# Second layer's first 512 MLP features by seven half-size products, with the first two products of three groups in the seam

## The chip, the cores and the metric

One core of one Trainium2 chip runs the whole program. The metric is the device time of one execution in microseconds (us). Differences of under 0.2% (1.6 us here) are not told from no change.

## The reference, cut to what matters

Two decoder layers work on 512 tokens of width 1024 in float32. Each has a mixer, a norm with a modulation that is computed from `c`, and an MLP of 4096 features. The second layer's mixer is a gated unit (called SGU below) that ends with the product by `sgu_w_out`. The change concerns the way from there into the second layer's MLP:

```python
def sq_relu_mlp(h, w1, w2):
    return jnp.square(jax.nn.relu(h @ w1)) @ w2
...
        x = x + g1[:, None, :] * y                                # y = gated @ w_out in layer 2
        h = modulate(rmsnorm(x, norm_mlp_g[i]), sh2, sc2)
        x = x + g2[:, None, :] * sq_relu_mlp(h, mlp_w1[i], mlp_w2[i])
```

## The kernel before

**Three products for one.** TensorE (PE) multiplies in a reduced float32 format. Each operand is split into a high part and a remainder (`wh`/`wl` for weights, two `hb` or `as` halves for activations), and a product is the sum of three matmuls (`mm3`, L558): `wl` by high, `wh` by remainder, `wh` by high, in this order for each slice of 128 inputs. So the second matmul of a product already needs the remainder of the activations. A weight split (`split`) is one ACT copy (`wh`) and one DVE subtraction (`wl`). `split_d` makes `wl` by two ACT copies and an accumulating DMA from POOL's queue in place of the subtraction; the list `LO` names the weights that are done so.

**The MLP's first matrix** is computed in eight groups of 512 features, called (c, j). A group is done either plainly (eight input slices, 512 tokens, 128 features at a time), or by seven half-size products (`s_prep`, `s_run`), the Winograd form of Strassen's scheme: inputs, features and tokens are halved, and each product m = 1 to 7 takes 512 inputs, 256 features and 256 tokens, that is 24 matmuls of 128x256. Products 1, 2 and 4 use plain quarters of the activations. Products 5, 6, 3 and 7 use sums of quarters (`a_parts`) that take both token halves. DVE builds them from `h32`, which holds the normed activations with features on partitions; then each is split into two halves (`as` or `hb`, function `parts`: an ACT copy and a DVE subtraction). The weights of 5 and 6 are running sums in `tr` (DVE adds the block `rg` or `yr`). The accumulators are evicted to `g` by ACT (`g<-po`) or DVE (`g<-g,po`), then squared by ACT.

**The seam.** The last product of the mixer (`sgu_w_out`) is done for the token tiles 0, 1, 2 and then 3. After tile 2, `normed(0, 1, 1)` turns the first two token tiles: 16 transposes into four `px` banks, DVE and ACT scale them into `h32` (`h<-px`, one half of each bank each), then `parts` makes `hb`. After tile 3 the same follows for the second token half, `normed(1, 1, 1)`, as soon as its sums of squares are there: DVE adds into `x`, ACT squares, DVE adds up (`sums`), POOL takes the power (`rr`), DVE and ACT scale rows (`xs`). Meanwhile PE needs work on the first token half alone. In the kernel before this is `first1` (L1818): the second layer's first group is done plainly, in halves of 256 tokens, four times 24 matmuls on the first half, with the second `normed` within them, then four times 24 on the second half. The other seven groups follow by seven products each (`FROM[1] = 1`), the first of them in `ORDER1`.

**What sets the order.** PE's order is the program's. All other engines' orders are made by a planner (`Plan.run`) which replays the recorded operations with its own costs and writes each engine's queue; so an edit of one stage can reorder DVE, ACT, POOL and SP from where it is first felt. Every recorded operation therefore has one line in the profile, L128. An engine works its queue strictly in that order.

**Buffers that matter:** `gq`, eight tiles of 8 KB for `g`, gates and modulation columns (`ada`); `w4`, three raw weight tiles; five pairs `wh`/`wl`; PSUM with four banks in pool `ps` (`px`, most `po`) and four in `xz`.

Of the kernel before, what the change touches and what calls it, by code (L numbers as in the profile page):

```python
# [14 lines left out]
P = 128  # L15
# [407 lines left out]
@with_exitstack  # L423
def decoder_kernel(ctx: ExitStack, tc: tile.TileContext, xtok, vecs, fgrow, ada0, ada1, pool_w, w1s, w1, w1f, w1b, w2, w_v, w_u, w_o, wsT, ws, bs, out):
    nc = tc.nc
# [106 lines left out]

    LO = "o0 o1 u5 u7 v41".split()

# [520 lines left out]

    ORDER1 = (1, 2, 5, 6, 3, 7, 4)

# [11 lines left out]

    FROM = (3, 1)  # L1070

    def mlp(i, first, extra, last, ending):
# [3 lines left out]
        if True:  # L1076
            g, y_ = {}, []
            early = [gq.tile([P, 2, D], F32, name="rg", tag="g")] if FROM[i] < 3 - i else []

# [26 lines left out]
            def f_prep(u):  # L1106
                c, f = u
                return split(raw4(w1[8 * c + f] if i == 0 else w1f[8 * c + f]))

# [11 lines left out]

            sums_a = {}

            x32 = h32[0] if i else xf

            def a_parts(step):


                def a(r, j):
                    return x32[:, 4 * j : 4 * j + 4, 256 * r : 256 * r + 256]  # L1130

                def operand(pool, tag):
                    o = pool.tile([P, 2, 4, 256], F32R, name="as", tag=tag)
                    return o[:, 0], o[:, 1]

                if step == 0:
                    first, half = slice(0, 256), slice(256, 512)
                    sums_a.update({1: H(slice(0, 4), first), 2: H(slice(4, 8), first), 4: H(slice(4, 8), half)})
# [18 lines left out]
            def blk(c, j, r, n):  # L1157
                if (c, j, r, n) not in blks:
                    q = quad_at(c, j) - quad_at(*first_quad)
                    if (r, n) == (1, 0):  # L1160
                        o = w4.tile([P, D], F32, name="raw", tag="w4")
                    elif (r, n) == (0, 0):
                        o = (chained or chained.append(hx.tile([P, 2, D], F32, name="tr", tag="t0")) or chained)[0][:, q % 2]
                    elif q == 0 and early:
                        o = early[0][:, r]
                    else:
                        o = (pieces or pieces.append(ytile("yr")) or pieces)[0][:, 2 * (q % 2) + r]
# [7 lines left out]
            def s_prep(u):  # L1175
# [22 lines left out]
                more = {1: [(c, j, 0, 1), (c, j, 1, 1)], 5: [(*nxt, 0, 0)], 6: [(c, j, 1, 0)], 3: [(*nxt, 0, 1)], 7: [(*nxt, 1, 1)]}.get(m, [])  # L1198
                for at in more:
# [6 lines left out]
            def s_run(u, w):  # L1206
# [5 lines left out]
                if start:  # L1212
                    banks[:] = [bank("po")]
                po = banks[0].rearrange("p (a t) -> p a t", a=2)
                wv = w[0].rearrange("p (k c) -> p k c", k=4), w[1].rearrange("p (k c) -> p k c", k=4)
                for f in range(2):
                    for k in range(4):
                        mm3(po[:, f], cut(wv, ALL, k, slice(P * f, P * f + P)), apart(cut(sums_a[m], ALL, k)), start and f + k == 0, stop and f + k == 4, skip_group_check=True)

# [157 lines left out]

            done = first(put)
            units = [("f", divmod(f, 8)) for f in range(done, 4 * FROM[i])]
            at = []  # L1380
            for q in range(FROM[i], 8):
                units += [("s", (*divmod(q, 2), m)) for m in (ORDER1 if q == FROM[i] < 3 - i else ORDER)]
                at.append(len(units) - 1)
# [76 lines left out]
    def normed(hf, i, n, xs=None, ks=range(0, KD, 2)):  # L1460
# [3 lines left out]
        for k in ks:  # L1464
# [5 lines left out]
            for q in range(2):  # L1470
# [346 lines left out]

    def first1(put):  # L1818
        n = 4
        wf = [split(raw4(w1f[f]), 1 if f else 4) for f in range(n)]  # L1820
        wf = [(h.rearrange("p (k c) -> p k c", k=KD), l.rearrange("p (k c) -> p k c", k=KD)) for h, l in wf]
        pos = [bank("po", xz) for _ in range(n)]
        for hf in range(2):
            c = slice(256 * hf, 256 * hf + 256)
            for f in range(n):
                if hf == 0 and f < 2:
                    mm3_late(pos[f][:, c], [cut(wf[f], ALL, k) for k in range(KD)], [apart(H(k, c)) for k in range(KD)])
                    continue
                for k in range(KD):
                    mm3(pos[f][:, c], cut(wf[f], ALL, k), apart(H(k, c)), k == 0, k == KD - 1)  # L1830
                    if (hf, f, k) == (0, n - 2, LATE):
                        normed(1, 1, 1)
                        spill(1)
        for f in range(n):
            put(f, pos[f].rearrange("p (r c) -> p r c", r=2))
        return n

    fgb = []
# [28 lines left out]

    ex = [x for q in range(8) for x in modulation_late(48 + q, 6 + 4 * q, late_gb if q == 0 else get_gb)]
    ex += [(49, lambda: spread_cols(mods[1][:, c_g(1, 0) : c_g(1, 0) + KD], "gain1"))]
    mlp(1, first1, ex, last1, lambda: None)  # L1870
    plan.run(LEAD)

# [12 lines left out]
def _lay_out(inp):  # L1885
# [35 lines left out]
    d["w1"] = fmajor(w1[0][:, : 3 * S], P)  # L1921
    d["w1f"] = fmajor(w1[1][:, : 1 * S], P)

    w1b = np.concatenate([w1[0][:, 3 * S :], w1[1][:, 1 * S :]], axis=1)
    d["w1b"] = w1b.reshape(2, 4, P, 12, 2, 256).transpose(3, 0, 4, 2, 1, 5).reshape(12, 2, 2, P, D)

# [27 lines left out]
```

## Time and profile before

| | |
|---|---|
| time, median of 3 runs | 800.47 us (799.83 to 800.86) |
| the profiled execution | 800.96 us |
| its span in the trace | 799.3 us |
| granted TensorE clock, mean | 0.994 |
| DVE busy | 690.7 us, 86% of the span |
| ACT busy | 531.7 us, 67% |
| seam: last matmul by `sgu_w_out` starts | 491.61 us |
| seam: second `normed`, 16 transposes start | 499.53 us |
| seam: first product with a sum of quarters (5) starts | 520.37 us |

The profile lists for each instruction its start, its length and, in brackets, how long its engine idled before it and what ended that. Successive instructions of one engine overlap a little, so the pitch from start to start counts as what one costs its engine. Matmuls of 128x256 read 0.27 us each but follow each other every 0.11 us.

### The profile page before, as it was taken

How to read it: one execution, taken by the hardware profiler on the slowest of the kernel's cores; microseconds unless marked ns; L12 is line 12 of the kernel's file. 1: busy time of each engine (PE TensorE's matmuls, PEld its weight loads, DVE VectorE, ACT ScalarE, POOL GpSimd, SP SyncE). 2: the span in 40 equal slices, each digit the busy share in tenths (PEclk: the TensorE clock that was granted, in tenths of full speed). 3: DMA queues.
4: the chain of work that ended last, by engine and by line, in shares of the span. 5: the costliest groups of instructions: out<-in, count | busy, mean ns of one | idle time of the engine just before them, and what ended most of it. 6: DMA issues, size and time to landing. Idle time of an engine off the chain costs nothing.

```text
span 799.3 us, 12696 instructions
## 1 busy us (share of the span) xinstructions
PE 781.3 (98%) x4893; PEld 708.4 (89%) x4893; DVE 690.7 (86%) x898; ACT 531.7 (67%) x768; POOL 106.3 (13%) x121
## 2 busy tenths in 40 slices
PE   5999999999999999999999999999999999999996
PEld 5778889999988888888889889999999998888885
DVE  5989799998789997999976998998878578898897
ACT  5486687776766666767677536877676686666672
POOL 4000001000010132152111101010001011012101
PEclk8999999999999999999999999999999999999999
DMA  9988959997999999427689974378775789999802
GB/s 342 417 316 311 354 194 285 276 277 205 324 289 242 230 246 255 181 109 208 157 269 310 309 299 159 131 202 278 232 209 161 197 255 279 198 228 207 216 1 105
DMA packets 48668, 189.14 MB, mean 237 GB/s; under 512 B 5440, under 2 KB 5600, under 8 KB 44768
## 3 DMA queue, kind: packets, MB, share of 16 engines
q1 hardware_dynamic: 36432, 128.81, 42.8%
q0 software_dynamic: 11744, 57.17, 35.2%
q10 hardware_dynamic: 432, 2.36, 0.7%
q8 instruction: 38, 0.62, 0.3%
q14 instruction: 22, 0.18, 0.1%
HBM read 181.49 MB, written 6.31 MB: 235 GB/s over the span
## 4 chain that ended last, share of the span: by engine, by line
PE 83%; DMA 6%; DVE 5%; issue 3%; ACT 3%; SPq 0%; POOL 0%; POOLq 0%; DVEq 0%; ACTq 0%
PE po L128 41%; PE pm L128 36%; PE po L100 2%; DMA ada<-in_ada 1%; DMA raw<-in_w 1%; PE px L100 1%; DMA wl<-in_w_o 1%; DMA x<-in_xtok 1%; PE pq L100 1%; DVE ada L100 1%; ACT wh L128 1%; DVE wl L128 1%; DMA yr<-in_w1b 1%; PE px L128 1%; ACT tmp L128 1%
## 5 line engine op out<-in xcount | busy, mean ns | idle before, releaser
L128 PE MATMUL pm<-wh,op 128*128 128x512 f32 x896 | 267.5, 379 | 0.0
L128 PE MATMUL po<-hb,wh 128*128 128x256 f32 (+1 forms) x1136 | 212.6, 291 | 0.0
L128 PEld LDWEIGHTS pm<-wh,op 128*128 128x128 f32 x896 | 169.4, 189 | 24.0
L128 PEld LDWEIGHTS po<-hb,wh 128*128 128x128 f32 x1136 | 178.0, 192 | 4.7
L128 PE MATMUL pm<-wl,op 128*128 128x512 f32 x448 | 169.9, 379 | 0.0
L128 PE MATMUL po<-hb,wl 128*128 128x256 f32 (+1 forms) x569 | 163.3, 292 | 0.0
L128 PEld LDWEIGHTS po<-hb,wl 128*128 128x128 f32 x569 | 107.8, 192 | 2.5
L128 PE MATMUL po<-as,wh 128*128 128x256 f32 x576 | 97.2, 275 | 0.0
L128 ACT ACTIVATE op<-g 128x1024 fp32r<-128x1024 f32 x56 | 59.1, 1056 | 56.9 <-PE pm L128 47.4
L128 PEld LDWEIGHTS pm<-wl,op 128*128 128x128 f32 x448 | 84.7, 189 | 12.1 <-DVE wl L128 0.3
L128 DVE TENSOR_TENSOR op<-g,op 128x1024 fp32r<-128x1024 f32 x56 | 68.3, 1221 | 24.5 <-ACT op L128 24.5
L128 PEld LDWEIGHTS po<-as,wh 128*128 128x128 f32 x576 | 87.5, 192 | 0.0
L128 DVE TENSOR_TENSOR wl<-bt,wh 128x1024 fp32r<-128x1024 f32 x64 | 78.1, 1231 | 9.1 <-ACT wh L128 9.0
L128 ACT ACTIVATE wh<-bt 128x1024 fp32r<-128x1024 f32 x64 | 67.1, 1050 | 20.5 <-PE pm L128 14.0
L128 PE MATMUL po<-as,wl 128*128 128x256 f32 x288 | 79.3, 275 | 0.3 <-ACT g L128 0.3
L128 DVE SCALAR_TENSOR_TENSOR ada<-ada,cb 128x1024 f32<-128x1024 f32 x56 | 67.8, 1219 | 7.4 <-DMA ada<-in_ada 7.4
L128 ACT ACTIVATE g<-g 128x512 f32<-128x512 f32 x100 | 61.2, 628 | 18.4 <-DVE g L128 17.3
L128 DVE TENSOR_TENSOR wl<-tr,wh 128x1024 fp32r<-128x1024 f32 x48 | 58.6, 1222 | 9.9 <-ACT wh L128 9.6
L128 ACT ACTIVATE wh<-tr 128x1024 fp32r<-128x1024 f32 x48 | 50.7, 1056 | 24.4 <-PE po L128 14.2
L128 DVE TENSOR_TENSOR wl<-raw,wh 128x1024 fp32r<-128x1024 f32 (+1 forms) x44 | 51.9, 1184 | 8.2 <-ACT wh L128 8.1
L128 PEld LDWEIGHTS po<-as,wl 128*128 128x128 f32 x288 | 55.3, 192 | 0.5 <-ACT g L128 0.5
L128 ACT ACTIVATE wh<-raw 128x1024 fp32r<-128x1024 f32 (+1 forms) x46 | 45.2, 996 | 15.8 <-PE po L128 7.8
(223 smaller groups left out, 1200.6 us busy)
## 6 DMA issues: line engine op xcount, KB each, us to landing
ada<-in_ada SPq DMA_DIRECT2D x76, 512.0 KB, 6.4
bt<-in_w POOLq DMA_DIRECT2D x22, 1024.0 KB, 9.9
yr<-in_w1b SPq DMA_DIRECT2D x22, 512.0 KB, 6.5
bt<-in_w SPq DMA_DIRECT2D x16, 512.0 KB, 8.1
b<-in_w SPq DMA_DIRECT2D x16, 512.0 KB, 9.8
raw<-in_w SPq DMA_DIRECT2D x13, 512.0 KB, 6.8
tr<-in_w1b SPq DMA_DIRECT2D x12, 512.0 KB, 6.1
raw<-in_w1b SPq DMA_DIRECT2D x12, 512.0 KB, 5.6
```

The lines of the kernel that those rows point to most:

```text
L100: return f(*a, **kw)
L128: self.ops.append((name, attr, lambda: f(*a, **kw), out, ins, kw))
```

## The change

The second layer's first 512 features are done by seven products too (`FROM[1] = 0`), and `first1` is gone with its weight layout `w1f`. To have work on the first token half while the second is normed, the products 1 and 2 (which need the first half alone) of three groups are done first: `SEAM` lists group and product (c j m), so 001 002 011 012 101 102, then the remaining five of each group interleaved. The second `normed` now stands within 011, after 57 matmuls of 128x256 (before: after 69).

```diff
-A_PARTS = ((0, 0, 1, 2, 7), (0, 0, 0, 1, 2))
+A_PARTS = ((0, 0, 1, 2, 7), (3, 4, 5, 6, 7))
-    LO = "o0 o1 u5 u7 v41".split()
+    LO = "o0 o1 o2 u5 u7 v41".split()
-    ORDER1 = (1, 2, 5, 6, 3, 7, 4)
+    LO1 = {(1, 0, 1), (1, 0, 2)}
+    SEAM = "001 002 011 012 101 102 005 006 003 007 015 004 016 013 017 105 014 106 103 107 104"
-    FROM = (3, 1)
+    FROM = (3, 0)
...
                 if step == 0:
+                    if i:
+                        s5 = get_gb().rearrange("p (k c) -> p k c", k=4)
+                        V.tensor_tensor(s5, a(1, 0), a(1, 1), ALU.subtract)
+                        V.tensor_tensor(a(1, 1), s5, a(0, 0), ALU.subtract)
+                        V.tensor_tensor(a(0, 1), a(1, 1), a(0, 1), ALU.add)
+                        V.tensor_tensor(a(1, 0), a(0, 0), a(1, 0), ALU.subtract)
+                        sums_a["t"] = {5: s5, 6: a(1, 1), 3: a(0, 1), 7: a(1, 0)}
+                        return
...
-                w = split(wb)
+                if i and u in LO1:
+                    w = split_d(wb, w1b[quad_at(c, j), *{1: (0, 0), 2: (1, 0), 3: (1, 1)}[m]])
+                else:
+                    w = split(wb, 4 if i and u == (0, 0, 1) else 1)
...
-                    banks[:] = [bank("po")]
+                    banks[:] = [bank("po", xz if i and quad_at(c, j) - quad_at(*first_quad) < 3 and m == 1 else None)]
...
+                        if i and (c, j, m) == (0, 0, 1):
...
+                            late.append((f, ws[1], ms[0]))
+                            continue
+                        mm3(po[:, f], ws, ms, start and f + k == 0, stop and f + k == 4, skip_group_check=True)
+                        if i and (c, j, m, f, k) == (0, 1, 1, 0, 2):
+                            normed(1, 1, 1)
+                            spill(1)
...
-            parts(H(slice(k, k + 2), c), tt)
+            if k > 3 or not (hf and n and h32):
+                parts(H(slice(k, k + 2), c), tt)
...
-    SEQ = "v1 v2 u0a c1 u1a r0 u0b v5 c1 u2 v6 c1 c1 v3 u1b c1 r1 u3 v7 c1 c1 n0 v4 c1 c1 n2 n3 c1 n1 u4 c1 u5 u6 c1 m1 m0 m2 c1 m3 g0 g1 m4 s0 g2 g3 m5 u7 g4 m7 m6 g5 g6 g7".split()
+    SEQ = "v1 v2 c1 u0a c1 u1a r0 u0b v5 c1 c1 u2 v6 c1 c1 v3 u1b r1 u3 v7 c1 c1 n0 v4 c1 c1 n2 n3 c1 n1 u4 c1 u6 c1 u5 m1 m0 m2 c1 m3 g0 g1 m4 s0 g2 m5 u7 g3 g4 m7 m6 g5 g6 g7".split()
...
-    ex = [x for q in range(8) for x in modulation_late(48 + q, 6 + 4 * q, late_gb if q == 0 else get_gb)]
+    ex = [x for q in range(8) for x in modulation_late(48 + q, 6 + 4 * q + 7, late_gb if q == 0 else get_gb)]
```

Apart from these, the tiles for `tr` and `rg` of the three groups come from `gq`, the second token half of the first 512 inputs is no longer split into `hb` by `normed` (its place is used by product 7), the weights of 101 and 102 are split by `split_d`, and so is the third weight tile of `sgu_w_out` (`o2`). In the mixer (`SEQ`) modulation columns (`c1`) come earlier, and `u6` goes ahead of `u5`.

Where the second `normed` stands, **DVE** before reads so (`x1` and `tmp_1519` are the last token tile, `px_1539` to `px_1542` the second half's banks):

```order
L128 TENSOR_SCALAR xs_1510<-x1_1266,rr_1538 128x1024
L128 TENSOR_SCALAR h32_1457<-px_1539,scl11_94,mods1_90 128x256
L128 TENSOR_SCALAR h32_1457<-px_1540,scl11_94,mods1_90 128x256
L128 TENSOR_SCALAR h32_1457<-px_1541,scl11_94,mods1_90 128x256
L128 TENSOR_TENSOR hb_1455<-h32_1457,hb_1453 128x2x256
L128 TENSOR_SCALAR h32_1457<-px_1542,scl11_94,mods1_90 128x256
```

and in the changed kernel, from the same row on to the remainder of product 5's sum (`as_1559`):

```order
L128 TENSOR_SCALAR xs_1510<-x1_1266,rr_1547 128x1024
L128 TENSOR_TENSOR g_1536<-g_1536,po_1541 128x512
L128 TENSOR_SCALAR h32_1457<-px_1548,scl11_94,mods1_90 128x256
L128 TENSOR_TENSOR tr_1520<-tr_1520,rg_1523 128x1024
L128 TENSOR_SCALAR h32_1457<-px_1549,scl11_94,mods1_90 128x256
L128 TENSOR_SCALAR h32_1457<-px_1550,scl11_94,mods1_90 128x256
L128 TENSOR_SCALAR h32_1457<-px_1551,scl11_94,mods1_90 128x256
L128 TENSOR_TENSOR rg_1523<-rg_1523 128x1024
L128 TENSOR_TENSOR ada_1555<-h32_1457 128x1024
L128 TENSOR_TENSOR wl_1543<-tr_1520,wh_1542 128x1024
L128 TENSOR_TENSOR hb_1456<-h32_1457,hb_1454 128x2x256 x2
L128 TENSOR_TENSOR as_1559<-ada_1555,as_1559 128x1024
```

The eviction of 002 (`po_1541`) and the weight sum for 005 (`tr`, `rg`) have come in between the scalings.

**ACT** at the same place, changed kernel (before, `xs` is followed at once by `h32<-px` and `hb<-h32` in turn):

```order
L128 ACTIVATE wh_1534<-tr_1533 128x1024
L128 ACTIVATE tmp_1519,sums_1499<-x1_1266 128x512
L128 ACTIVATE xs_1510<-x1_1266,rr_1546 128x1024
L128 ACTIVATE wl_1535<-tr_1533 128x1024
L128 ACTIVATE g_1536<-po_1537 128x512
L128 ACTIVATE wl_1540<-raw_1538 128x1024
L128 ACTIVATE wh_1539<-raw_1538 128x1024
L128 ACTIVATE h32_1457<-px_1548,mods1_90,scl11_94 128x256
L128 ACTIVATE g_1536<-g_1536 128x512
L128 ACTIVATE h32_1457<-px_1549,mods1_90,scl11_94 128x256
L128 ACTIVATE h32_1457<-px_1550,mods1_90,scl11_94 128x256
L128 ACTIVATE h32_1457<-px_1551,mods1_90,scl11_94 128x256
```

Three copies for 101 and 102 (`wl_1535`, `wl_1540`, `wh_1539`) and an eviction now stand between `xs` and the first `h32`.

**DVE** goes on, in the changed kernel, through the operands of 006 (`wl_1554`, `as_1564`), 003 (`wl_1558`, `as_1568`) and 007 (`wl_1563`, `hb_1455`), with the weight sum of 015 (`rg_1529`) before the last:

```order
L128 TENSOR_TENSOR tr_1520<-tr_1520,rg_1523 128x1024
L128 TENSOR_TENSOR h32_1457<-ada_1555,h32_1457 128x4x256
L128 TENSOR_TENSOR h32_1457<-h32_1457 128x4x256
L128 TENSOR_TENSOR wl_1554<-tr_1520,wh_1553 128x1024
L128 TENSOR_TENSOR as_1564<-h32_1457,as_1564 128x1024
L128 TENSOR_TENSOR wl_1558<-rg_1523,wh_1557 128x1024
L128 TENSOR_TENSOR as_1568<-h32_1457,as_1568 128x1024
L128 TENSOR_TENSOR h32_1457<-h32_1457 128x4x256
L128 TENSOR_TENSOR wl_1563<-rg_1523,wh_1562 128x1024
L128 TENSOR_TENSOR tr_1520<-tr_1520,rg_1529 128x1024
L128 TENSOR_TENSOR hb_1455<-h32_1457,hb_1453 128x4x256
```

Before, the same operations end with `hb_1455` too; there PE stands between the second `normed` and product 5 in 27 + 96 matmuls of the plain group and the products 1 and 2 of one group, now in 15 matmuls of 011 and the products 012, 101 and 102.

More of the change, by code (lines that the diff above doesn't have):

```diff
@@ L1077, in mlp @@
             g, y_ = {}, []
-            early = [gq.tile([P, 2, D], F32, name="rg", tag="g")] if FROM[i] < 3 - i else []
+            early = []
             def y(t, dh):
@@ L1162, in blk @@
                     elif (r, n) == (0, 0):
-                        o = (chained or chained.append(hx.tile([P, 2, D], F32, name="tr", tag="t0")) or chained)[0][:, q % 2]
-                    elif q == 0 and early:
-                        o = early[0][:, r]
+                        if i and q in (0, 2):
+                            chained[:] = [gq.tile([P, 2, D], F32, name="tr", tag="g")]
+                        elif q == 4 * i:
+                            chained[:] = [hx.tile([P, 2, D], F32, name="tr", tag="t0")]
+                        o = chained[0][:, q % 2]
+                    elif i and q < 2:
+                        if len(early) == q:
+                            early.append(gq.tile([P, 2, D], F32, name="rg", tag="g"))
+                        o = early[q][:, r]
                     else:
@@ L1217, in s_run @@
                     for k in range(4):
-                        mm3(po[:, f], cut(wv, ALL, k, slice(P * f, P * f + P)), apart(cut(sums_a[m], ALL, k)), start and f + k == 0, stop and f + k == 4, skip_group_check=True)
+                        ws, ms = cut(wv, ALL, k, slice(P * f, P * f + P)), apart(cut(sums_a[m], ALL, k))
+                        if i and (c, j, m) == (0, 0, 1):
+                            T.matmul(po[:, f].rearrange("p (s h) -> p s h", h=2), ws[0], ms[0], start=f + k == 0, stop=False, skip_group_check=True)
+                            T.matmul(po[:, f].rearrange("p (s h) -> p s h", h=2), ws[0], ms[1], start=False, stop=False, skip_group_check=True)
+                            late.append((f, ws[1], ms[0]))
[4 more added lines that the diff above has]
+                            spill(1)
+                for f, w_, m_ in late:
+                    T.matmul(po[:, f].rearrange("p (s h) -> p s h", h=2), w_, m_, start=False, stop=False, skip_group_check=True)
                 def block(r, n):
@@ L1376, in evict @@
                     last(t, 0, S, po)
-            done = first(put)
+            done = first(put) if first else 0
             units = [("f", divmod(f, 8)) for f in range(done, 4 * FROM[i])]
             at = []
-            for q in range(FROM[i], 8):
-                units += [("s", (*divmod(q, 2), m)) for m in (ORDER1 if q == FROM[i] < 3 - i else ORDER)]
+            if i:
+                units += [("s", tuple(int(x) for x in u)) for u in SEAM.split()]
+                at.append(len(units) - 1)
+            for q in range(3 if i else FROM[i], 8):
+                units += [("s", (*divmod(q, 2), m)) for m in ORDER]
                 at.append(len(units) - 1)
@@ L1816, in decoder_kernel @@
                     spill(0)
[L1818 to L1836, printed above, removed]
     fgb = []
```

22 lines of the change are left out of this document (10 added, 12 removed).

## The prediction

> **What bounds the kernel now.** First the busy times, then what PE waited for, then the chain of work that ended last, then a window of the steady part.
>
> ```profile
> PE 781.3 (98%) x4893; PEld 708.4 (89%) x4893; DVE 690.7 (86%) x898; ACT 531.7 (67%) x768; POOL 106.3 (13%) x121
> ```
>
> ```profile
> PE po L128 <- DMA wl<-in_w_o: 0.5, 1, 0.5
> PE px L128 <- ACT xs L128: 0.4, 1, 0.4
> PE po L128 <- DVE v L128: 0.2, 1, 0.2
> ```
>
> ```profile
> 486.81 12.88 PE po L128 x93
> 499.69 1.75 PE px L128 x16
> 501.44 142.38 PE po L128 x1275
> ```
>
> ```profile
> 540.00:560.00 20.00, 20.00 (x181) 20.00 (x180) 15.91 (x19) 14.71 (x21) 1.69 (x2) 1.00 0.88 281
> ```
>
> PE is busy 98% of the span. The three waits are all that it has in the last 460 us, 1.1 us together, and the chain stays on PE through the seam and for the 142 us behind it. In the window (first PE, then DVE with 15.91 us and ACT with 14.71 us of 20; 1.00 is the granted clock) PE issues 181 matmuls of 128x256 in 20 us, 0.1103 us each. So the time falls by each matmul that goes, as long as the others still deliver; 24 matmuls, one half-size product, take 2.65 us. The trace has room on DVE on average, but what counts is the seam.
>
> **Term 1, PE's work.** `first1` is 4 blocks of 128 features, 8 input slices, 3 matmuls, two token halves: 192 matmuls of 128x256. In its place stand seven products of 24: 168. The order of instructions confirms 24 fewer. 24 x 0.1103 = **-2.65 us**.
>
> **Term 2, the end of the mixer.**
>
> ```profile
> 450.04 0.48 PE L128 MATMUL po<-wl,gt 128*128 128x512 f32 x1 [0.45 <-DMA wl<-in_w_o]
> L128 PE MATMUL po<-wl,gt x33: 379/379/483, 448.1 to 469.6; 128*128 128x512 f32 x33
> 439.40 0.87 POOL L128 DMA_DIRECT2D wl<-in_w_o  x1 [9.38 <-PE po L128]
> 441.30 0.86 POOL L128 DMA_DIRECT2D wl<-in_w_o  x1 [1.02 <-ACT wl L128]
> 417.21 11.44 SPq L128 DMA_DIRECT2D ada<-in_ada  x6
> 428.75 15.11 SPq L128 DMA_DIRECT2D raw<-in_w_o  x5
> 447.36 1.22 DVE L128 TENSOR_TENSOR wl<-raw,wh 128x1024 fp32r<-128x1024 f32 x1
> ```
>
> PE idles 0.45 us for the accumulating DMA of `o1`, issued at 441.30 and landed at 450.0. SP issues `w_o` loads behind six `ada` loads that take 11.44 us; with the columns moved forward in `SEQ` three stand there, so `raw` of `o0` and `o1` comes earlier, and the wait should go: **-0.45 us**. `o2` loses its DVE subtraction at 447.36 and gets a third accumulate. If the three followed each other at the pitch of now (439.40 to 441.30, 1.90 us, and 8.7 us to landing), it would land at 451.9; the first `wl` matmul is at 448.1 and the second was wanted at 449.6, so the third at about 451.1. The bounds are -0.45 and +0.8; I take the first, as all three start earlier.
>
> **Term 3, the seam.** PE's side comes first.
>
> ```profile
> 491.61 0.38 PE L128 MATMUL po<-wh,gt 128*128 128x512 f32 x1
> 499.53 1.91 PE L128 MATMUL px<-ident,xs 128*128 128x128 f32 x16
> 520.37 0.28 PE L128 MATMUL po<-as,wl 128*128 128x256 f32 x1
> 528.41 0.28 PE L128 MATMUL po<-hb,wl 128*128 128x256 f32 x1
> ```
>
> On the clock of before, the mixer ends at 491.83. Transposes then come after 57 matmuls (001, 002, 9 of 011): 491.83 + 57 x 0.1103 = 498.1, in place of 499.53; with 1.75 us for them, 15 matmuls and three products, 005 is due at 509.5, 006 at 512.1, 003 at 514.8 and 007 at 517.4. Before, product 5 starts 28.5 us behind the mixer, now 17.6 us: DVE and ACT have 10.9 us less to build the sums. The remainder `hb` of product 7 was ready early:
>
> ```profile
> 522.80 1.22 DVE L128 TENSOR_TENSOR hb<-ada,hb 128x1024 fp32r<-128x1024 f32 x1
> 505.69 1.22 DVE L128 TENSOR_TENSOR ada<-h 128x1024 f32<-128x1024 f32 x1
> 506.82 1.22 DVE L128 TENSOR_TENSOR h<-h 128x1024 f32<-128x1024 f32 x1
> 495.06 0.68 DVE L128 TENSOR_TENSOR x<-x,tmp 128x512 f32<-128x512 f32 x1
> 500.17 1.45 DVE L128 TENSOR_SCALAR h<-px,scl,mods 128x256 f32<-128x256 f32 x3 [1.45 <-PE px L128]
> 490.16 2.97 ACT L128 ACTIVATE wh<-raw 128x1024 fp32r<-128x1024 f32 x3
> 511.41 0.58 ACT L128 ACTIVATE g<-po 128x512 f32<-128x512 f32 x1
> ```
>
> It ended at 524.0, 4.4 us before PE took it at 528.41. 10.9 us less is 6.5 us too little, unless DVE sheds work: about 3 us of it go. That already says some 3 us of waiting. The walk gives it row by row. Pitches from the rows: DVE 1.135 us for 1024 elements (505.69 to 506.82), 0.60 for 512, 0.455 for an `h` (three in 1.45); ACT 0.95 for a copy of 1024 (three in 2.97, less their overlap), 0.53 for an eviction.
>
> When are `xs` there?
>
> ```profile
> 482.80 0.21 DVE L128 TENSOR_SCALAR sums<-sums 128x1 f32<-128x1 f32 x1
> 484.14 0.76 DVE L128 TENSOR_SCALAR xs<-x,rr 128x1024 f32<-128x1024 f32 x1 [0.46 <-POOL rr L128]
> 495.78 0.63 ACT L128 ACTIVATE tmp<-x 128x512 f32<-128x512 f32 x1 [1.61 <-DVE x L128]
> 497.97 0.75 DVE L128 TENSOR_SCALAR xs<-x,rr 128x1024 f32<-128x1024 f32 x1 [0.85 <-POOL rr L128]
> ```
>
> Before, the last token tile's `x` was done at 495.7 and `xs` at 498.7. Now one weight split less stands in DVE's way there, `x` ends at 494.4, ACT squares behind its weight copies by 495.4, sums stand at 495.5, and 1.34 us later (482.80 to 484.14) `xs` starts: done at 497.6. PE needs it at 498.1, so the earlier transposes wait for nothing, with 0.5 us to spare.
>
> Then DVE's queue, in the order shown with the change. The eviction of 002 waits for ACT's copy of 001, which stands behind `xs` and a weight copy: 498.0 to 498.6. First `h` at 498.75 (0.64 us behind the transposes' start, as at 500.17 against 499.53); weight sum to 500.34. ACT meanwhile does two copies, 1.9 us, and only then its `h` of the first bank, a square, and the other three `h`, which DVE's wait for: DVE idles 1.0 us, its other three `h` run from 501.36 to 502.74. From here it is one chain of DVE: `rg` 503.9, sum of 5 at 505.0, `wl` 506.1, two `hb` 507.3, `as` of 005 508.5. PE wants that at 509.6: no wait. Five operations on, `as` of 006 is done at 514.1, wanted 512.2: PE waits **1.9 us**. `as` of 003 is done at 516.4, in time. Four on, `hb` of 007 at 520.95, wanted 519.4 after the first wait: **1.5 us** more. Together **+3.4 us**. Behind 007 come 015 and 004, whose operands exist by then.
>
> The waits are not a sum of all delays but the latest delivery against PE's plan (520.95 - 517.5), so bounds are simple. With no DVE idleness from `xs` on (0.5 + 0.15 + 1.0 us) and `xs` 0.25 us earlier, 1.5 us; with ACT 1.3 us later than I take it, which passes through the `h` to everything, 4.7 us. I take the walk.
>
> One row carries the 1.0 us of idleness, the wait for a shared bank:
>
> ```profile
> 500.75 0.56 ACT L128 ACTIVATE h<-px,mods,scl 128x256 f32<-128x256 f32 x1 [2.14 <-DVE h L128]
> ```
>
> Here ACT stood 2.14 us and started when DVE had read its half of that `px` bank, though both halves had long been written. The Trainium skill, in "PSUM — Partial Sum Buffer", section "PSUM bank collisions raise a hardware error ⚠️", says that two engines may not touch one bank at a time, two reads included, and must be kept apart by a dependency. The trace agrees with its 2.14 us; without such a rule DVE would not idle for ACT, the seam would cost 2.4 us and the sum be 799.8.
>
> The accumulating loads for 101 and 102 are hidden in the walk:
>
> ```profile
> tr<-in_w1b POOLq DMA_DIRECT2D x12, 512.0 KB, 5.5
> wl<-in_w_o POOLq DMA_DIRECT2D x2, 512.0 KB, 7.8
> xd<-x POOLq DMA_DIRECT2D x2, 1024.0 KB, 5.4
> ```
>
> POOL can issue them at 497.5 and 498.9, behind a spill at 494.6 (5.4 us to landing). At 5.5 us they land by 504.4, wanted at 504.2 and 506.8; at 7.8 the first is 1.1 us late. That delay is no addition: PE then stands early instead of at 006, and the delivery of 007 sets the total all the same.
>
> **Sum.** 800.96 (the profiled execution) - 2.65 - 0.45 + 3.4 = 801.3. That execution lies 0.49 above the median, so **800.8 us**.
>
> **Rivals.**
>
> *A, the forecast:* seam waits of 1.5 to 4.7 us eat the gain: 798.9 to 802.1, within 0.2% (1.6 us) of before, which is about what a measurement can tell from no change. Chance 0.47.
>
> *B, DVE keeps up:* idleness in DVE's queue does not occur, because ACT gets through its two copies earlier, and 006's and 007's remainders come 2 us ahead of the walk. Seam 0 to 1.5 us: 797.4 to 798.9, faster. For it: the walk's DVE idleness rests on ACT's place alone, and PE without waits gives the full 3.1 us. Against: even a DVE that never idles is late at 007. Chance 0.34.
>
> *C, slower:* the weights of 101 are loaded into a `gq` tile that the last modulation column frees.
>
> ```profile
> 481.25 1.22 DVE L128 SCALAR_TENSOR_TENSOR ada<-ada,cb 128x1024 f32<-128x1024 f32 x1
> tr<-in_w1b SPq DMA_DIRECT2D x12, 512.0 KB, 6.1
> raw<-in_w_v SPq DMA_DIRECT2D x2, 512.0 KB, 15.6
> ```
>
> So that load starts at 482.4, and its copy `wh_1534` stands in ACT's queue ahead of the last token tile's square. At 6.1 us it lands at 488.5, harmless. From a landing 11 us after issue (493.4) on it holds the square, `xs`, the transposes and everything behind; at 15.6 us it lands at 498.0, and the transposes come about 4 us later: 804.8. Chance 0.19.
>
> That the change doesn't remove what it says is excluded by the order: 24 matmuls fewer.
>
> **Numbers.** The range goes from a seam without waits, 797.4, to most of C, 803.6. Faster is B, 0.34; same is A, 0.47; slower is C, 0.19.
>
> **What would show it.** In the profile after: 24 matmuls fewer; no wait for `wl<-in_w_o`; product 5 starting 17.6 us behind the mixer; PE waits `po <- DVE as` of 1.9 us at 006 and `po <- DVE hb` of 1.5 us at 007; DVE idle before its second `h` for ACT's. I am wrong if 006 and 007 start without waits (B), if `px` waits for `xs` (C), or if waits appear outside the seam, in the mixer or behind 007.

## The result and the profile after

The changed kernel takes 805.51 us (804.36 to 808.75), before 800.58 us beside it: 1.0069 times, 95% interval 1.005 to 1.0089. A second measurement on another chip gave 804.85 against 801.74 us, 1.0037 (1.0021 to 1.0054). So it is slower by 3 to 5 us; forecast was no change, 800.8 us. The page of the changed kernel (the profiled execution took 807.32 us, its span is 805.6 us) has PE's work down as forecast, 24 matmuls, but the span up:

```profile
PE 779.7 (97%) x4869; PEld 705.8 (88%) x4869; DVE 693.1 (86%) x901; ACT 536.7 (67%) x775; POOL 100.0 (12%) x126
```

PE's waits in it, longest first (total, times, longest; the first three lines of before's list, which are from the start of the program, stand here too and are left out):

```profile
PE po L128 <- DMA wl<-in_w1b: 1.8, 2, 1.0
PE po L128 <- DMA wl<-in_w_u: 1.3, 1, 1.3
...
PE pm L128 <- DVE op L128: 1.0, 1, 1.0
PE po L128 <- ACT g L128: 0.9, 1, 0.9
PE po L128 <- DVE hb L128: 0.6, 1, 0.6
```

The wait for `wl<-in_w_o` is gone, as forecast. In its place stands one for `wl<-in_w_u`; the seam waits for transfers; and there are waits behind the seam, where none was forecast. To see which of these waits stay, the start times of four matmuls that every kernel has are compared, two profiles of each (us): the transposes ahead of the mixer, the first matmul of the MLP, the first `wl` matmul of the MLP's second matrix, and the last matmul.

| | before | before_again | changed | after_again |
|---|---|---|---|---|
| the profiled execution | 800.96 | 803.07 | 807.32 | 802.41 |
| transposes ahead of the mixer | 367.65 | 368.52 | 369.57 | 366.77 |
| **mixer**, from there to the MLP | 124.2 | 125.4 | 125.1 | 125.5 |
| **first matrix** of the MLP | 152.0 | 152.0 | 154.2 | 152.5 |
| **second matrix** | 147.4 | 147.4 | 148.7 | 148.0 |

The means of the two pairs differ by 0.1, 0.5, 1.3 and 1.0 us, 2.9 us together, as the executions do. The forecast in these terms was -0.45 for the mixer, -2.65 + 3.4 = 0.75 for the first matrix and nothing for the second.

**The seam** in the changed kernel: the first rows of the MLP, where the mixer ends, PE's rows that idled, and the first product with a sum (start, length, and in brackets the idle time before and what ended it):

```profile
494.71 1.95 PE L128 MATMUL po<-hb,wh 128*128 128x256 f32 x16
...
508.17 0.38 PE L128 MATMUL po<-hb,wl 128*128 128x256 f32 x1 [0.83 <-DMA wl<-in_w1b]
...
512.10 0.35 PE L128 MATMUL po<-hb,wl 128*128 128x256 f32 x1 [0.98 <-DMA wl<-in_w1b]
...
514.85 0.28 PE L128 MATMUL po<-as,wl 128*128 128x256 f32 x1
523.74 0.49 PE L128 MATMUL po<-hb,wh 128*128 128x256 f32 x2 [0.57 <-DVE hb L128]
```

Product 005 starts 20.1 us behind the mixer, 17.6 us was due: 2.5 us went, 2.3 of them on the weights of 101 and 102, then 0.57 us on the remainder for 007. (A wait costs more than its idle time. Here 0.83 us of idle time moved the next matmuls by 1.1 us: matmuls overlap, idle time counts from the end of the last one, and the first pitch behind the wait is 0.21 us in place of 0.11. The difference is called a restart below.) That is 3.1 us, and 3.1 in the second profile too; forecast was 3.4. The wait of 1.9 us at 006 did not come: PE reached it 2.5 us later than planned, and its operand was there. DVE's two rows to look at are its wait for ACT's `h` and the remainder for 007:

```profile
503.87 1.46 DVE L128 TENSOR_SCALAR h<-px,scl,mods 128x256 f32<-128x256 f32 x3 [0.47 <-ACT h L128]
...
522.46 1.22 DVE L128 TENSOR_TENSOR hb<-h,hb 128x1024 fp32r<-128x1024 f32 x1
```

The transfers that PE waited for were issued by POOL so (the last line is from issue to landing):

```profile
500.32 0.92 POOL L128 DMA_DIRECT2D wl<-in_w1b  x1 [0.28 <-PE po L128]
501.75 0.86 POOL L128 DMA_DIRECT2D wl<-in_w1b  x1 [0.50 <-ACT wl L128]
...
DMA to landing us min/median/max: 7.8/9.0/10.2
```

**Behind the seam** the first profile lost 1.6 us more. A load for the next group is late, ACT's copy `wh<-tr` stands in its queue waiting for it, and the eviction behind that copy holds up PE (the first line is that load):

```profile
541.31 0.85 POOL L128 DMA_DIRECT2D tr<-in_w1b  x1 [8.32 <-DVE wl L128]
...
549.34 1.06 ACT L128 ACTIVATE wh<-tr 128x1024 fp32r<-128x1024 f32 x1 [1.79 <-DMA tr<-in_w1b]
...
550.91 0.57 ACT L128 ACTIVATE g<-po 128x512 f32<-128x512 f32 x1
...
551.54 0.38 PE L128 MATMUL po<-hb,wl 128*128 128x256 f32 x1 [0.85 <-ACT g L128]
```

The load landed 8.0 us after its issue. Four profiles issue it at the same distance from the mixer, 46.4 to 46.7 us: this one, after_again, and those of spill_late and u5_first below. It took 8.0 and 8.3 us in the two where PE waits (here and u5_first), 6.2 and 6.4 us in the two where it does not. So this loss comes and goes with one landing; at this order a landing of 8 us is too late:

```profile
546.77 1.06 ACT L128 ACTIVATE wh<-tr 128x1024 fp32r<-128x1024 f32 x1 [2.65 <-DMA tr<-in_w1b]
...
545.11 1.06 ACT L128 ACTIVATE wh<-tr 128x1024 fp32r<-128x1024 f32 x1
```

(ACT's copy in u5_first, then in after_again, where ACT did not idle.)

**At the second matrix** PE (its accumulator is `pm`) waits for the remainder of its activations (`op`), DVE for ACT's half of them:

```profile
661.79 1.23 DVE L128 TENSOR_TENSOR op<-g,op 128x1024 fp32r<-128x1024 f32 x1 [0.82 <-ACT op L128]
663.07 0.48 PE L128 MATMUL pm<-wh,op 128*128 128x512 f32 x1 [0.99 <-DVE op L128]
```

ACT starts that `op` 10.9 us behind the first matmul of this matrix (659.77 against 648.90 us); before it was 9.5 us (653.32 against 643.87). Four squares `g<-g` stand ahead of it in ACT's queue in place of two, and they waited 2.7 us for DVE's evictions. The planner made another order there too. The second profile has the same order there and loses 0.6 us.

**The mixer**: POOL issues the accumulating transfer for `u5` at 424.83 us (before: 414.11), and PE stands for it. Before, it landed at 424.09 us, 1.0 us ahead of the product that needs it. The lines are the issue and the first matmul of `u5`, before and then changed:

```profile
414.11 0.86 POOL L128 DMA_DIRECT2D wl<-in_w_u  x1 [3.00 <-ACT wl L128]
425.12 0.38 PE L128 MATMUL po<-hb,wl 128*128 128x512 f32 x1
...
424.83 0.86 POOL L128 DMA_DIRECT2D wl<-in_w_u  x1 [12.06 <-ACT wl L128]
433.83 0.45 PE L128 MATMUL po<-hb,wl 128*128 128x512 f32 x1 [1.34 <-DMA wl<-in_w_u]
```

Counted from the transposes ahead of the mixer, the issue is 8.8 us later (55.26 against 46.46 us), and the product is due only 5.3 us later (62.8 against 57.5 us), about one product's time.

### The profile page after: what moved, and what is told of

The parts are those of the page before. It is cut to its first block, busy times and chain, and to the rows that moved or that the text cites. A ratio compares the mean times of both kernels' runs of the same rounds, so it can differ in the third digit from the quotient of the medians.

```text
span 805.6 us, 12667 instructions
## 1 busy us (share of the span) xinstructions
PE 779.7 (97%) x4869; PEld 705.8 (88%) x4869; DVE 693.1 (86%) x901; ACT 536.7 (67%) x775; POOL 100.0 (12%) x126
## 4 chain that ended last, share of the span: by engine, by line
PE 72%; DMA 12%; DVE 7%; ACT 4%; issue 3%; SPq 0%; POOL 0%; POOLq 0%; ACTq 0%; DVEq 0%
PE pm L128 34%; PE po L128 32%; PE po L100 4%; DVE wl L128 2%; ACT wh L128 2%; DMA bt<-in_w 2%; DMA ada<-in_ada 2%; DMA vb<-in_w_v 2%; DMA tr<-in_w1b 2%; DMA wh<-in_ada 1%; DMA wl<-in_w_u 1%; DMA x<-in_xtok 1%; DMA wl<-vb 1%; PE pq L100 0%; ACT wl L128 0%
## 5 line engine op out<-in xcount | busy, mean ns | idle before, releaser
L128 PE MATMUL po<-hb,wh 128*128 128x256 f32 (+1 forms) x1072 | 203.0, 292 | 0.6 <-DVE hb L128 0.6
L128 PEld LDWEIGHTS po<-hb,wh 128*128 128x128 f32 x1072 | 168.9, 192 | 5.5 <-DVE hb L128 0.8
L128 PE MATMUL po<-hb,wl 128*128 128x256 f32 (+1 forms) x537 | 156.2, 294 | 4.3 <-DMA wl<-in_w1b 1.8
L128 PE MATMUL po<-as,wh 128*128 128x256 f32 x624 | 105.3, 275 | 0.0
L128 PEld LDWEIGHTS po<-as,wh 128*128 128x128 f32 x624 | 94.9, 192 | 0.0
L128 DVE TENSOR_TENSOR wl<-bt,wh 128x1024 fp32r<-128x1024 f32 x64 | 77.2, 1218 | 10.9 <-ACT wh L128 10.9
L128 PE MATMUL po<-as,wl 128*128 128x256 f32 x312 | 85.8, 275 | 0.0
L128 DVE TENSOR_TENSOR wl<-tr,wh 128x1024 fp32r<-128x1024 f32 (+1 forms) x54 | 62.6, 1163 | 15.7 <-ACT wh L128 15.3
L128 ACT ACTIVATE wh<-tr 128x1024 fp32r<-128x1024 f32 (+1 forms) x55 | 55.1, 1008 | 25.7 <-PE po L128 15.9
L128 ACT ACTIVATE wh<-raw 128x1024 fp32r<-128x1024 f32 x40 | 41.9, 1052 | 23.0 <-PE po L128 19.0
L128 DVE TENSOR_TENSOR wl<-raw,wh 128x1024 fp32r<-128x1024 f32 x36 | 45.3, 1267 | 6.4 <-ACT wh L128 6.3
```

What stands on the lines that cost most here:

```text
L128: self.ops.append((name, attr, lambda: f(*a, **kw), out, ins, kw))
```

## The experiments

Ratios are to the kernel before, beside it on the same chip, with 95% intervals.

### Both kernels again

**after_again** (no edit).

> The changed kernel once more, for a second profile. In the first one the time over the forecast lies in four places: 1.9 us before 210 us, where the order of instructions is that of before; 0.96 us lost in the mixer where 0.45 us of gain were forecast; 1.6 us of waits behind product 007; 1.3 us at the start of the second MLP matrix. Theory: the first of these is a matter of the execution and goes (matmul at 211.8 us back near 209.8 us), the other three are the kernel's and stay within 0.4 us each. Rival: all of them are landings of transfers that differ from run to run; then each of them changes by 0.5 us or more.

804.85 us, 1.0037 (1.0021 to 1.0054). The early 1.9 us went, so they were of that execution. PE's waits:

```profile
PE po L128 <- DMA wl<-in_w1b: 2.1, 2, 1.2
PE po L128 <- DMA wl<-vb: 1.1, 1, 1.1
...
PE pm L128 <- DVE op L128: 0.3, 1, 0.3
PE po L128 <- DVE hb L128: 0.2, 1, 0.2
```

Of the waits that the changed kernel added, those for the two transfers in the seam are as long again; `hb` and `op` are shorter by 0.3 and 0.7 us, the one in the mixer is for another transfer (the mixer took 125.5 us all the same), and those for `g` behind the seam are missing. So of the four places the theory holds for the start alone; behind 007 and at the second matrix the rival does, and the mixer kept its time by another wait.

**before_again** (no edit).

> The kernel before once more, for a second profile. So far the mixer took 124.2 us in the one profile of before, and 125.1 to 127.7 us in five profiles of changed kernels, with waits for accumulating transfers (wl<-vb, wl<-in_w_u) that come and go at the same order of instructions. Theory 1 (these waits are a matter of the single execution, before's too): the mixer takes 124.5 us or more here, with such a wait. Theory 2 (they are due to the changed kernels): 124.2 us within 0.2 us, and no such wait.

0.9995 (0.9982 to 1.0009). The mixer took 125.4 us with a wait of 1.8 us for `wl<-vb`: theory 1. Waits for `wl<-vb` belong to the execution, of whatever kernel.

### The mixer

**mixer_old**

```diff
-    LO = "o0 o1 o2 u5 u7 v41".split()
-    SEQ = "v1 v2 c1 u0a ... u4 c1 u6 c1 u5 m1 ...
+    LO = "o0 o1 u5 u7 v41".split()
+    SEQ = "v1 v2 u0a c1 ... u4 c1 u5 u6 c1 m1 ...
```

> The changed kernel with the mixer's order SEQ and the list LO of before. Theory (the mixer's new order costs 1.4 us against the forecast, by the wait for the accumulating transfer of u5): 0.45 us of the old wait come back and 1.5 us of new ones go, so about 1.0 us faster than the changed kernel, 804.5 us. Rival (the wait is a late landing of that execution, and the new order is good for 0.45 us): 0.5 us slower, 806.0 us.

807.96 us, 1.007 (1.0052 to 1.0089). Neither: the mixer took 125.7 us, as long as in the changed kernel, but the first matrix 158.7 us, with waits of 2.9 us for DVE's `g` and 0.8 us for the last `xs`. So the mixer's order and list can't be undone by themselves there. They were next put into the kernel before.

**mixer_new**: before with `LO` and `SEQ` of the changed kernel.

> The kernel before with the mixer's new order SEQ and the new list LO, its MLP unchanged. Theory 1 (the order of the mixer costs nothing by itself, its transfers' landings vary): within 0.7 us of before; no wait for wl<-in_w_o. Theory 2 (the new order costs 1 to 1.4 us in the mixer by the transfers for u5 and u6): 1 us slower than before. From the first matmul of the MLP to its last nothing changes by either, since DVE had 4.4 us to spare there.

804.96 us, 1.0036 (1.0022 to 1.005): slower, as theory 2 had it, but by 2.9 us in place of 1. Its one profile fell on its fastest execution, 802.0 us.

**mixer_new_again** (the same).

> mixer_new once more, for a second profile, since its first one fell on its fastest run (802.0 us against a median of 805.0 us) and showed only 0.7 us of wait for wl<-in_w_u. Theory 1 (u5's late transfer): a wait for wl<-in_w_u of 1 to 2 us and a mixer of 125.5 to 127 us in a run near the median. Theory 2: the mixer is as in the first profile, 124.4 us, and the time is lost behind it, by waits for DVE g.

1.0044 (1.0029 to 1.0059); the profiled execution took 807.8 us. Its mixer took 127.0 us, with 1.1 us of wait for `wl<-in_w_u` and 1.8 us for `wl<-vb`; 1.3 us for DVE's `g` (an eviction) came 43 us into the first matrix. Both theories have a part.

```profile
PE po L128 <- DMA wl<-vb: 1.8, 1, 1.8
PE po L128 <- DVE g L128: 1.3, 1, 1.3
PE po L128 <- DMA wl<-in_w_u: 1.1, 1, 1.1
```

**mixer_new_u5**

```diff
-... u4 c1 u6 c1 u5 m1 ...
+... u4 c1 u5 c1 u6 m1 ...
```

> The kernel before with the mixer's new order and LO, but u5 ahead of u6 as before; the MLP unchanged. mixer_new, with u6 first, was 3.1 us slower than before. Theory 1 (u6 ahead of u5 is the loss): within 0.6 us of before, the mixer at 124.2 to 125.4 us. Theory 2 (the columns moved forward, or o2's accumulating transfer, are the loss): 2 us or more slower than before, as mixer_new.

1.002 (1.0009 to 1.0031), between the two: by the ratios the swap is worth 0.16 to 0.24%, 1.3 to 1.9 us (the intervals overlap a little), and the rest of the new order and list still costs 0.2%. Its profile has no wait for `wl<-in_w_u` and a mixer of 124.8 us, but 0.9 us for DVE's `g` behind it. All three profiles of this MLP with the new order have that wait, 0.9 to 1.3 us at the same place, and neither of the two with the old order has it. Whether it comes from the columns or from `o2`'s transfer was not tested.

**u5_first**: the same swap in the changed kernel.

> The changed kernel with u5 ahead of u6 again in SEQ, all else as changed. Six of seven profiles with u6 first show a wait for the accumulating transfer wl<-in_w_u (0.6 to 1.6 us), none of three with u5 first. Theory 1 (u5's transfer is issued late, at 424.8 us in place of 414.1, because u5 was put behind u6): that wait goes, the mixer takes 124.2 to 125.4 us in place of 125.9 on the mean, and the kernel is 0.8 to 1 us faster than the changed one (about 804.0 us). Theory 2 (another part of SEQ): the wait or one for wl<-in_w_o or DVE's hs takes its place, and the time is the same within 0.5 us.

805.02 us, 1.0051 (1.0036 to 1.0067). The wait went and the mixer took 124.2 us, yet the ratio lies between the changed kernel's two: the first matrix took 154.4 us, with 1.6 us of waits for ACT's `g`, behind the load that landed late in this execution (shown above). Alone, the swap back brings no gain here that these intervals could show.

Over all profiles, a wait for `wl<-in_w_u` of 0.6 to 1.9 us stands in nine of ten with u6 first, and in none of ten with u5 first (seven with the rest of the new order, three with the old one). The mixer took 126.2 us on the mean with u6 first, 125.2 with u5 first. The waits for `wl<-vb` are as long in both groups (0.95 and 0.98 us on the mean), so they do not make this difference.

### The seam

**seam_dve**

```diff
-    LO1 = {(1, 0, 1), (1, 0, 2)}
+    LO1 = set()
```

> The changed kernel with LO1 empty: DVE splits the weights of 101 and 102, and POOL's two accumulating transfers go. Theory 1 (the seam is lost to DVE's chain up to the remainder of 007; the transfers only shift where PE stands): the two waits for wl<-in_w1b of 1.8 us go, but 2.3 us of DVE work come in ahead of 006 and 007, so the seam's waits grow by about 2.3 us in total, at 006 and 007: 807.8 us. Theory 2 (the seam is lost to the accumulating transfers): 2.4 us faster, 803.1 us.

810.03 us, 1.0101 (1.0083 to 1.012): theory 1, and 2 us more than it priced. 005 starts 17.8 us behind the mixer, on time, and then PE waits for DVE at 006:

```profile
515.64 0.35 PE L128 MATMUL po<-as,wl 128*128 128x256 f32 x1 [1.62 <-DVE wl L128]
516.68 0.80 PE L128 MATMUL po<-as,wh 128*128 128x256 f32 x2 [0.69 <-DVE as L128]
```

1.0 us more follow at 007, and 2.8 us in three evictions further back. Product 015, the first behind 007, starts 34.3 us behind the mixer, against 31.7 in the changed kernel: 2.6 us, near the 2.3 us of the two splits that DVE does more. So the seam came out as theory 1 priced it, and the surplus is in the evictions. DVE's queue has no room: take the transfers away, and their work and more comes back as waits for DVE.

**pairs**

```diff
-... 101 102 005 006 003 007 015 004 016 013 017 105 ...
+... 101 102 005 015 006 016 003 007 013 017 004 105 ...
```

> The changed kernel with the products that share an operand side by side (005 015 006 016 003 007 013 017 004 ...), so that 2.65 us of PE work lie between 005 and 006 and 5.3 us more ahead of 007. Theory 1 (DVE's chain of sums is late against PE's plan): the wait at 007 goes, 0.8 us with its restart, and no new one at 006, so 804.7 us. Theory 2 (weights are what is late: 015 and 016 need weight sums by DVE earlier): a wait of 1 to 2 us moves to 015 or 016, 805.5 to 807 us.

804.13 us, 1.0023 (1.001 to 1.0036). In this run 003 is added to the accumulator of 015, so its sums are wrong; the amount of work is the same, and pairs2 has them right. No wait for DVE in the seam, 2.3 us for `wl<-in_w1b`: theory 1.

**pairs2**: the same with

```diff
-            XS, ZS = {}, []
+            XS, ZS = {}, {}
-                banks = XS.setdefault((c, j), []) if m in IN_X else ZS
+                banks = XS.setdefault((c, j), []) if m in IN_X else ZS.setdefault((c, j), [])
```

> The products that share an operand side by side (005 015 006 016 003 007 013 017 004 ...), as in the run pairs, with the accumulator that products 5 and 3 share kept apart for each group (there 003 was added to the accumulator of 015). Theory 1 (DVE's lateness is over by this order, the transfers of 101 and 102 remain): waits in the seam for wl<-in_w1b alone, 0.5 to 1 us faster than the changed kernel. Theory 2 (an accumulator more that is held makes products wait for a free bank): waits po <- ACT g or DVE g in the seam of 1 us or more, no faster than the changed kernel.

803.93 us, 1.0024 (1.001 to 1.0038): theory 1. The first matrix took 151.7 us, and 1.6 us of waits for `wl<-in_w1b` were all in the seam.

**spill_late**

```diff
                             normed(1, 1, 1)
-                            spill(1)
+                        if i and (c, j, m, f, k) == (1, 0, 2, 1, 3):
+                            spill(1)
```

> The changed kernel with the spill of the second token half (1 MB on POOL's queue, at 497.5 us in the first profile, 2.8 us ahead of the accumulating transfers for 101 and 102) moved behind product 102. Theory 1 (the spill's traffic holds these transfers up): they land in 5.5 us, the wait for wl<-in_w1b falls from 2.1 us to under 0.8 us; DVE's wait at 007 then grows by what of the 3.4 us is not yet lost, about 0.5 us, so about 1 us faster than the changed kernel. Theory 2 (they are late because POOL issues them behind ACT's copies, at 500.3 and 501.8 us, and any transfer with accumulation takes 8 us here): the wait stays above 1.5 us, the time the same within 0.5 us.

1.004 (1.0027 to 1.0053), the wait 2.4 us. But the planner left the spill ahead of the two transfers on POOL (498.48 against 501.29 us), so this run tells nothing of either; one_u5 below bears on it.

**pairs2_early**: pairs2 with `LO1 = {(0, 1, 1), (0, 1, 2)}`.

> pairs2 with the accumulating transfers given to 011 and 012, in place of 101 and 102, whose weights DVE then splits. Theory 1 (with the sums side by side, what is left of the seam's loss is the two late transfers): no wait for wl<-in_w1b; from the mixer's end to the MLP's second matrix 149.5 to 150.2 us in place of 151.7; 2 us faster than pairs2, 802 us. Theory 2 (DVE is the seam's limit whatever the order): DVE's two splits, 2.3 us, come back as waits for DVE (wl or as) of 1.5 us or more, and the time is that of pairs2 within 0.7 us.

1.0071 (1.0048 to 1.0093). Neither: 011's transfer, issued at 496.07 us, was itself late, and PE stood 3.2 us for it at 504.33, then 1.6 us for `hb`.

**pairs2_dve**: pairs2 with `LO1 = set()`.

> pairs2 without accumulating transfers in the seam (LO1 empty): DVE splits the weights of 011, 012, 101 and 102. The same step cost the changed kernel's order 4.9 us. Theory 1 (the pairs leave DVE 2.65 us more at 006 and 5.3 us more at 007): waits for wl<-in_w1b go, one of at most 1.2 us for as at 005 comes; 0.5 to 1.5 us faster than pairs2. Theory 2 (the planner's order behind it, evictions held up by DVE, decides): 2 us or more slower than pairs2, with waits po <- DVE g or ACT g.

1.0074 (1.0056 to 1.0093): 4 us slower than pairs2, as theory 2 had it, but most of the waits are for DVE's operands: 1.1 us for `wl` and 0.7 for `as` at 006, 1.6 for `hb` at 007, and 1.3 us for ACT's `g`.

**pairs2_u5**: pairs2 with u5 ahead of u6.

> pairs2 with u5 ahead of u6 in SEQ: if both effects are real and independent, 0.8 to 1 us faster than pairs2; if the mixer's order works only through what it leaves to the seam, no faster, and other waits appear in the seam.

800.22 us against 800.85, 0.9995 (0.9985 to 1.0005); pairs2 was 1.0024. On top of the pairs the swap gains 0.29%, 2.3 us, more than expected, while in the changed kernel (u5_first) no gain could be told. PE's waits in it behind 400 us are these, no wait for u5's transfer among them:

```profile
PE po L128 <- DMA wl<-in_w1b: 1.9, 2, 1.0
...
PE px L128 <- DVE xs L128: 0.3, 1, 0.3
PE po L128 <- DVE v L128: 0.2, 1, 0.2
PE po L128 <- DMA wl<-vb: 0.2, 1, 0.2
```

**one_u5**: pairs2_u5 with `LO1 = {(1, 0, 2)}`; **mix_u5**: with `LO1 = {(0, 1, 2), (1, 0, 2)}`.

> pairs2_u5 with one accumulating transfer in the seam (102) in place of two; DVE splits the weights of 101. In pairs2_u5 the two transfers land 8.3 and 10.8 us after issue and cost two waits of 1.9 us, 2.4 us with restarts. Theory 1 (two transfers close together are late, one lands in 8 us or less; the pairs leave DVE over 1.1 us): no wait for wl<-in_w1b, at most 0.5 us for DVE; 2 us faster than pairs2_u5. Theory 2 (DVE has no room even for one split): waits for wl, as or hb by DVE of 1.5 us or more, no faster.

> pairs2_u5 with the two accumulating transfers given to 012 and 102 (each second product of its group), so that they stand apart and DVE's work is the same. Theory 1 (they are late because they come together, and 012's copies are there early): the waits for wl<-in_w1b fall under 0.6 us in all and the kernel is 1.5 to 2.4 us faster than pairs2_u5. Theory 2 (012's transfer is as late for its product as 011's was in pairs2_early, 3.2 us): a wait of 1 us or more at 012 and no gain.

1.0081 (1.0051 to 1.0111) and 1.0047 (1.0031 to 1.0062). In one_u5 neither theory holds: PE waits for no operand by DVE in the seam, but the one transfer left was issued later and took as long as each of two:

```profile
503.08 0.93 POOL L128 DMA_DIRECT2D wl<-in_w1b  x1 [4.44 <-ACT wl L128]
...
512.30 0.55 PE L128 MATMUL po<-hb,wl 128*128 128x256 f32 x1 [3.31 <-DMA wl<-in_w1b]
...
DMA to landing us min/median/max: 9.1/9.1/9.1
```

In mix_u5 012 waited 2.8 us: theory 2. So closeness is not the cause: such a transfer took 7.7 us or more in every profile, also alone and also behind the spill (in one_u5 the spill was issued at 496.12 us and had landed at 501.58). Each place tried left the first of them less time than that ahead of its product: 4.9 us at 011, 6.3 at 012, 6.9 at 101.

**spread**: pairs2_u5 with

```diff
-    LO1 = {(1, 0, 1), (1, 0, 2)}
+    LO1 = {(1, 0, 1)}
-... 101 102 005 015 006 016 003 007 013 017 004 105 ...
+... 101 005 102 015 006 016 003 013 007 017 004 105 ...
```

**pairs2_u5_again** (pairs2_u5, beside it).

> pairs2_u5 with its two remaining limits taken apart: 102 goes behind 005 and its weights are split by DVE (LO1 holds 101 alone), and 013 goes ahead of 007, so that the sum for 007 has 2.65 us more. Theory 1 (transfer of 101: 1.1 us; remainders of 005, 006, 003 and 007 in time): one wait for wl<-in_w1b of about 1 us, nothing for DVE, 1.3 us faster than pairs2_u5. Theory 2 (DVE's queue was just in time in pairs2_u5, so each split more comes back as a wait): waits for as or hb of 1 us or more, no faster than pairs2_u5.

> pairs2_u5 once more, on the same chip as spread. If its 800.2 us was its own and not that chip's: within 0.1% of before again, waits for wl<-in_w1b of 1.5 to 2 us as the only ones in the seam. If it was chance: 0.3% or more slower than before, as the changed kernel.

801.08 us for spread, 802.62 for pairs2_u5_again, 802.12 for before: 0.9993 (0.9982 to 1.0004) and 1.0005 (0.9994 to 1.0016). So pairs2_u5 is level with before again. In spread one wait for each limit is left:

```profile
506.82 0.38 PE L128 MATMUL po<-hb,wl 128*128 128x256 f32 x1 [1.03 <-DMA wl<-in_w1b]
...
529.25 0.49 PE L128 MATMUL po<-hb,wh 128*128 128x256 f32 x2 [0.53 <-DVE hb L128]
```

Theory 1 holds but for the 0.5 us for DVE. The 1.3 us that it expected over pairs2_u5 are not excluded: 1.0 us by the ratios, with intervals that overlap. No kernel here is faster than before beyond its interval.

## Why the prediction was wrong

- **PE's work, -2.65 us: right.** 24 matmuls fewer; one product takes 2.68 us in the traces.
- **The seam, +3.4 us: right in size** (3.1 us in both profiles), **not in its first releaser.** The walk gave the accumulating transfers 5.5 us, by the row of `tr`, with 7.8 us from the row of `wl` as the other end; they took 7.8 and 10.2. The trace of before had nearer rows, the accumulating transfers into `wl` for `u5` and `u7`, with 10.0 and 8.3 us. So PE stood at 101 and 102, product 005 came 2.5 us late, and the wait at 006 that was named as a sign was not there. As the prediction said, such a delay is no addition: 007's remainder was ready at 523.7 us, 29.0 behind the mixer, and the walk had 29.1 (520.95 - 491.83). seam_dve shows DVE's limit without the transfers (but with two splits more for DVE), pairs2 the transfers without DVE's.
- **DVE idle for ACT's `h`, 1.0 us:** 0.47 us. Right in kind, with half the size. The row that was to carry it was read too high: of the 2.14 us that ACT stood before, all but 0.6 us passed before that bank was written, for its first matmul started at 499.53 us, DVE's `h` at 500.17 and ACT's at 500.75. In the changed kernel the bank had been written for over a microsecond when DVE's 0.47 us began. The rule of the Trainium skill that was weighed there ("PSUM — Partial Sum Buffer", section "PSUM bank collisions raise a hardware error ⚠️") agrees with that row: DVE's `h` stands until ACT has read its half of the bank.
- **The mixer, -0.45 us: wrong, the step that failed first.** Put alone into the kernel before, the new order and list cost 0.36 and 0.44%, 2.9 to 3.5 us, in place of a gain (mixer_new twice). The step followed the loads of `w_o` alone and has no word on the swap of `u5` and `u6`. `u5` has an accumulating transfer too: it is issued 8.8 us later and its product is due only 5.3 us later, so the 1.0 us that it had to spare became a wait of 0.6 to 1.9 us in nine of ten profiles. The swap costs 1.3 to 1.9 us in mixer_new and 1.5 to 2.3 in pairs2 (1.0024 to 0.9995 and 1.0005). The rest goes with the wait for DVE's eviction in the first matrix; which part of the new order brings it is open. The upper bound of +0.8 was put on the wrong transfer, `o2`. The -0.45 itself rested on one execution: the wait for `wl<-in_w_o` went in every profile of the new order, but before_again and mixer_old, with the old order, don't have it either; there PE had waited 1.8 and 1.6 us for `wl<-vb` ahead of it.
- **"Behind 007 come 015 and 004, whose operands exist by then": wrong, the step that failed second.** It costed all behind the seam at nothing. The operands of these two were there, but a load for the group after them had no room, and evictions came late behind it: 1.6 us in one profile of two, 2.8 us in seam_dve. And the second matrix lost 1.3 and 0.6 us, in an order that the prediction had not looked at. No run takes this loss away by itself.
- **Rival C** had the slower side for another reason, a late load of 101's weights; `px` stood 6.4 us behind the mixer as planned, so it did not happen. Its time, 804.8 us, is near by chance.
- **The range** ended at 803.6. It was made of the seam's bounds and most of rival C; nothing was set aside for the two places above.

With u5 first and the pairs, the kernel comes level with before (0.9995, 1.0005), so these two are enough to make up the miss in the median. How the loss divides between them in the changed kernel is not settled: there u5_first alone showed no gain, as its first matrix was 154.4 us long. At best 0.5 us of the 2.65 us came out: the first matrix took 151.5 us in spread and 151.8 in pairs2_u5, against 152.0 before, and what is left in spread are the two waits shown, one for a transfer and one for DVE, 1.6 us without their restarts.

## What to carry over

When a change shortens the work that covers a chain, compare the cover with the chain's length first: 10.9 us less cover against 4.4 us of slack and some 3 us of work shed told the seam's loss to within 0.4 us. Then follow each moved step's own transfers to their deadline, and read the new order of every queue to the end of the program where a planner makes it: the terms that were missed stood outside the seam. Two limits that are about equally late have to be taken away together: with the transfers gone the waits came back at DVE (seam_dve), with DVE's gone the transfers stayed (pairs2). And a wait that is found in one profile is worth looking for in a second one of the same kernel before a gain is booked for it.

## What was not expected of the hardware

- Accumulating transfers of 512 KB from `in_w1b` into a `wl` tile landed 7.7 to 11.3 us after issue, in the thirteen profiles that have them; those from `in_w_u`, in the mixer, took 7.4 to 10.7 us in twenty profiles. Those from `in_w1b` into a `tr` tile took 5.0 to 9.3 us, 5.5 in the median of 255. The runs don't show why.
- At one order of PE's, ACT's and POOL's instructions, executions differ: the transposes ahead of the mixer started between 366.8 and 370.1 us in twenty profiles (366.8 and 369.6 us in the two of the changed kernel), and the wait for `wl<-vb` was between nothing and 2.0 us.
